# Unused pieces of 64 and 96 bytes between SBUF tiles in a decoder step: where matmul operands start modulo 128

## The chip, the cores and the metric

The kernel runs on one NeuronCore of one Trainium2 chip. The metric is the device time of one execution in microseconds (us). The engines are named as in the profile: PE is TensorE's matmul, PEld its weight load, DVE is VectorE, ACT is ScalarE, POOL is GpSimd, SP is the engine whose queue issues the DMAs. SBUF is the on-chip memory of 128 partitions; a tile has an address within the partition, the same in all 128, and that byte address is what this document is about.

## The reference

One inference step of a one-layer decoder, for 1024 prompt tokens and 64 sample tokens (8 sequences of 8), in float32:

```python
h = rmsnorm(x, norm_mix)
q, k, v, gu, gv, ga, gb = split_in(h @ w_in)          # 1024 -> 5120 columns
o  = sink_attention(q, k, v, ...)                     # window 128, 16 heads, 4 key heads
vn = layernorm(gelu(gv), ln_g, ln_b)
s  = spatial_gating(gelu(gu), vn, ws, bs)             # 6 groups of 128x128
x  = x + (sigmoid(ga) * (o @ w_pa) + sigmoid(gb) * (s @ w_pb)) @ w_out
z  = rmsnorm(x, norm_ffn) @ w_up                      # 1024 -> 5632 columns
c  = conv_b + sum(zp[:, j:j + T] * conv_w[j] for j in range(3))
a, b = split(c, 2)
y  = rmsnorm(x + (gelu(a) * b) @ w_down, norm_final)  # 2816 -> 1024
```

The outputs are y for both groups, the new key, value and convolution states, and vn of the samples.

## The kernel before

**Three products for one.** Every large operand is held as two float32r tiles, a high part and the remainder (th and tl, wh and wl, hh and hl). A float32 product is made of three matmuls, high by high, high by low and low by high, accumulated in PSUM. Each matmul loads its own 128x128 weights; the other operand, the moving one, has 256, 288, 320 or 512 columns of 4 bytes.

**Two token groups.** Group 0 holds the 64 samples and 512 prompt tokens (576), group 1 the other 512.

**The stages, in order of time**, each with its matmul line:

- Token-major projections (L511, in mm_tok): gv and v. Here the hidden state is the weights operand (pools hs0 for group 0, hs1 for group 1) and the projection's weights are the moving operand, 256 columns, in pool wide. Group 0 has 5 token blocks, group 1 has 4, each for 4 column blocks of 24 matmuls: 480 and 384 matmuls.
- The combined projection (L295, in Chain.product): q, k, gu and the gates, in 16 column pairs. A pair is a 2x2 block product in 7 products instead of 8, each of 12 matmuls for a group: group 0 with 288 columns from pool T0h, group 1 with 256 columns from pool T1h, 16 x 84 = 1344 matmuls each. Three pairs run for group 0 alone at the start of the stage and for group 1 alone at its end; between them the groups alternate, twelve matmuls of one and twelve of the other.
- Attention for group 0, then group 1 (scores L1155 with kst as moving operand and q as weights, both in pool kv; transposes L1182; values L1206), with pieces of the branch and merge products (L238, in mm3) put between the steps. L238 of group 0 runs 320 and 256 columns in turn (pools mlp0, act0, later hm0), of group 1 512 columns (mlp1, act1, later hm1).
- The merge of group 1 and the output projection (L238, hm0 from 726 to 776 us, hm1 from 784 us).
- The up-projection (L295 again, psu banks): 22 column pairs, group 0 with 288 columns from pool T0, group 1 with 256 columns from pool T1, 22 x 84 = 1848 matmuls each. DVE and ACT make the weight parts (L41, L177) and run the convolution (L1532 to L1534) beside it.
- The down-projection (L1651, in mm_dn): 7 passes over 11 column pairs, three matmuls of 288 columns and three of 256 in turn, both from pool tq; 924 of each.

The weights of L295, L238 and L1651 come from ring buffers in pool wp, made by ACT (high part) and DVE (low part) at L41.

**Where a tile lies.** A pool on the left side is put at the end of the left pools open at that moment; one on the right side is put below those open on the right. Inside a pool, a name's buffers are put one after another when the name is first used, in steps of 32 bytes. So what comes into a left pool moves all later names of that pool, and all pools opened on the left while it is open; the right pools (hs0, T0h, mlp0, act1, vv1, T0, tq) stay. An address is taken again by a later pool when a pool closes; the first access to the new tile then waits for the last accesses to the old tiles it overlaps.

Nearly all tile sizes are multiples of 128 bytes, so a pool's start decides the address modulo 128 of all its operands. wp starts at byte 2336, which is 32 modulo 128, and each of its matmul operands is at 32. The columns "before" are the addresses in the built program before; "after" adds the bytes of the diff by the rule above. Distance is moving operand less weights, modulo 128.

| matmuls | columns | weights | moving operand | distance before | after |
|---|---|---|---|---|---|
| L511, group 0 (480) | 256 | hs0, 96 | wide, byte 113024: 0 | 32 | 64 (wide at 32) |
| L511, group 1 (384) | 256 | hs1, byte 78208: 0 | wide: 0 | 0 | 64 (hs1 at 96, wide at 32) |
| L295, group 0 (1344) | 288 | wp, 32 | T0h, 96 | 64 | 64 |
| L295, group 1 (1344) | 256 | wp, 32 | T1h, byte 70016: 0 | 96 | 64 |
| L238, group 0, branch (288) | 320, 256 | wp, 32 | mlp0, 96 | 64 | 64 |
| L238, group 1, branch (144) | 512 | wp, 32 | mlp1, byte 145792: 0 | 96 | 64 |
| L238, group 0, merge (384) | 320, 256 | wp, 32 | act0, byte 70016: 0 | 96 | 64 |
| L238, group 1, merge (192) | 512 | wp, 32 | act1, 96 | 64 | 64 |
| L238, group 0, output (384) | 320, 256 | wp, 32 | hm0, byte 102784: 0 | 96 | 64 |
| L238, group 1, output (192) | 512 | wp, 32 | hm1, byte 70016: 0 | 96 | 64 |
| L1155 (224) | 256 | q in kv, 0 | kst in kv, byte 106880: 0 | 0 | 64 (kst at 96, q at 32) |
| L1206, group 0 (56) | 512 | vv0, 0 | at0, 32 | 32 | 96 |
| L1206, group 1 (64) | 512 | vv1, 96 | at1, 32 | 64 | 96 |
| L295, up, group 0 (1848) | 288 | wp, 32 | T0, 96 | 64 | 64 |
| L295, up, group 1 (1848) | 256 | wp, 32 | T1, byte 55584: 32 | 0 | 64 |
| L1651 (924 and 924) | 288, 256 | wp, 32 | tq, 96 | 64 | 64 |

**The lines the steps touch.** The matmul that most of the span consists of is in Chain.product:

```python
for kk in range(4):
    th, tl = (x[:, (0, 1, 2, 6, 3, 5, 4)[j]] for x in self.tx[kk])
    for i, (u, v) in enumerate(((wh, th), (wh, tl), (wl, th))):
        PE.matmul(ps, u[:, kk, :], v, start=first and kk + i == 0,
                  stop=kk == 3 and i == 2, skip_group_check=True)
```

Its moving tiles are made here for group 1, in the combined projection and in the up-projection:

```python
txa[1][kk] = tuple(t1h.tile([P, 7, 256], F32R, name=f"t{y}{kk}") for y in "hl")
tx[1][kk] = tuple(t1p.tile([P, 7, 256], F32R, name=f"t{y}1{kk}") for y in "hl")
```

The pools around the change are c1 (small constants and statistics, open during everything up to the up-projection), wide, kv, mlp1 and T1. All DMAs of these stages go through the queue of SP; the order on each engine is the order of the program text.

Of the kernel before, what the change touches and what calls it, by code (L numbers as in the profile page):

```python
# [6 lines left out]
F32 = mybir.dt.float32  # L7
# [8 lines left out]
P = 128  # L16
# [18 lines left out]
def layer(tc, a):  # L35
# [13 lines left out]
    with ExitStack() as top:  # L49
# [191 lines left out]
        W = Weights(top.enter_context(tc.tile_pool(name="wp", bufs=2)), 4, 4)  # L241
        W.sm = top.enter_context(tc.tile_pool(name="sm", bufs=2))

        tx = [{}, {}]
        tops = ExitStack()

# [2 lines left out]
        def right(stack, name, bufs=1):  # L249
            return stack.enter_context(tc.tile_pool(name=name, bufs=bufs, side="right", reuse_waits="tile"))  # L250
# [110 lines left out]
        with ExitStack() as ph1:  # L361
            c1 = ph1.enter_context(tc.tile_pool(name="c1", bufs=1))
# [31 lines left out]
            wide = {}  # L394
# [68 lines left out]

            rstg = [c1.tile([P, len(gr["toks"])], F32, name=f"rst{gr['g']}") for gr in groups]
            lnst = c1.tile([P, 9, 3, 6], F32, name="lnst")
            pso = ExitStack()
            psa = pso.enter_context(tc.tile_pool(name="psa", bufs=7, space=PSUM))

# [25 lines left out]
            gvp = pa0.enter_context(tc.tile_pool(name="gvp", bufs=4))  # L494
            hp1 = pa0.enter_context(tc.tile_pool(name="hs1", bufs=1))
            wide["pool"] = pa0.enter_context(tc.tile_pool(name="wide", bufs=2))
            hp0 = right(hs0o, "hs0")
            rsg = [pool.tile([P, gr["n"]], F32, name=f"rs{gr['g']}") for gr, pool in zip(groups, (c1, hp1))]
            hs = [[], []]
# [390 lines left out]
            kvo, kvp = ExitStack(), {}  # L890
# [3 lines left out]
            def operands(gr, kv):  # L894

                def go():
                    if kv == NKV:
                        if gr["g"] == 0:
                            operands(groups[1], 0)()
                        return  # L900
                    g, n = gr["g"], gr["n"]
                    at, nk = ((NS, 512), (448, 640))[g]
                    t = kvp["p"].tile([P, 2, 640], F32R, name="kst", bufs=2)[:, :, :nk]
                    gr["kst"][kv] = t
                    r = 64 * (kv % 2)
                    for o in (0, 64):
                        nc.sync.dma_start(t[o:o + 64].bitcast(F32), kd[kv // 2][r:r + 64, :, at:at + nk])
                    for c in (2 * kv, 2 * kv + 1):
                        q = gr["qt"][c] = kvp["p"].tile([P, 2, 512], F32R, name="q", bufs=4)
                        nc.sync.dma_start(q.bitcast(F32), qd[g][c][:, :, gr["soff"]:n])  # L910
                return go

            def prepare(gr):

                g = gr["g"]
                gr["kvo"] = ExitStack()
                vp = (gr["kvo"].enter_context(tc.tile_pool(name="vv0", bufs=1, reuse_waits="tile")) if g == 0
                      else right(gr["kvo"], "vv1"))
                gr["vst"], gr["dvst"] = {}, {}

                def value(name, src, i):
                    def go():
                        t = gr[name][i] = vp.tile([P, NKV, P], F32R, name=f"{name}{i}")
                        nc.sync.dma_start(t.bitcast(F32), src[i])
                    return go

                vs, ds = (((0, 1, 2), (1, 2, 3)), ((3, 4, 5, 6), (4, 5, 6, 7)))[g]
                return [operands(gr, 0)] * (1 - g) + [value("vst", vd, vs[0])] + [
                    x for i in range(len(ds)) for x in (
                        [value("vst", vd, vs[i])] * (i > 0) + [value("dvst", dvd, ds[i])])] + [operands(gr, 1)]  # L930
# [44 lines left out]
            kvp["p"] = kvo.enter_context(tc.tile_pool(name="kv", bufs=1, reuse_waits="tile"))  # L975
            prep = prepare(groups[0])
            m1 = mo[1].enter_context(tc.tile_pool(name="mlp1", bufs=1, reuse_waits="tile"))
            b_order = [(0, 0), (1, 0), (0, 1), (1, 1)] + [(c, g) for c in range(2, KD) for g in range(2)]
            sgs, bst = {}, {}

# [465 lines left out]
        def pool2(name, bufs, **kw):  # L1446
            return ph2.enter_context(tc.tile_pool(name=name, bufs=bufs, reuse_waits="tile", **kw))

        t1p = pool2("T1", 1)
        up = pool2("up", 2)  # L1450
        pse = ExitStack()
        psu = pse.enter_context(tc.tile_pool(name="psu", bufs=8, space=PSUM, reuse_waits="tile"))
# [437 lines left out]
```

## Time and profile before

| | |
|---|---|
| median of 3 runs | 1540.58 us (1537.99 to 1541.20) |
| the profiled execution | 1540.43 us, span 1538.7 us, granted clock 0.998 |
| PE busy, share of the span | 1524.6 us, 99%, 11528 matmuls |
| DVE busy | 1178.6 us, 77% |
| ACT busy | 851.4 us, 55% |
| DMA queue of SP, share of 16 engines | 55.3% |

A profile's matmul record runs from the start of a matmul to the modelled end of its results, and the next one starts long before. A group's "mean ns" is the length of that record. How fast matmuls follow one another is seen from a stretch of time and the number of matmuls in it, or from the starts in the timeline. A row of the view by stretches gives the stretch, its length, for each engine its busy time and number of instructions, then the granted clock, the share of the DMA engines and GB/s. A row of groups gives line, engine, operation, output and inputs, shape and count, then busy time and mean, then idle time before.

### The profile page before, as it was taken

The page shows a single profiled execution, that of the slowest core. Times are in us where ns is not written, and L with a number is a line of the kernel's source. Part 1 is how long each engine was busy: PE and PEld are TensorE (multiplying, and loading weights), DVE is VectorE, ACT ScalarE, POOL GpSimd, SP SyncE. Part 2 cuts the span into 40 slices and gives each one's busy share as a digit, 9 for nine tenths or more (in the row PEclk, how much of TensorE's full clock was granted, in tenths as well). Part 3 has the DMA queues.
Part 4 walks back from the last instruction along what each step waited for, and adds up shares of the span by engine and source line. Part 5 has one row for each costly group of instructions (what it writes and reads, how often), then busy time and mean ns, then how long its engine had stood idle before and what let it go on. Part 6 is the DMA issues. An engine that isn't in the chain of part 4 may idle for free.

```text
span 1538.7 us, 30106 instructions
## 1 busy us (share of the span) xinstructions
PE 1524.6 (99%) x11528; PEld 1483.3 (96%) x11528; DVE 1178.6 (77%) x1897; ACT 851.4 (55%) x1767; POOL 267.8 (17%) x382
## 2 busy tenths in 40 slices
PE   9999999999999999999999999999999999999997
PEld 8999999999998989988989999999999999999997
DVE  7798876755576877979568978898898878775686
ACT  7557666653455775764444554655555556453452
POOL 0001000110030222310234222332142222000002
PEclk9999999999999999999999999999999999999999
DMA  7687446764778757449977423332232216973363
GB/s 244 219 270 260 161 161 218 236 212 142 241 237 285 221 165 252 152 140 312 339 255 267 138 109 113 121 120 93 108 128 100 102 62 224 365 252 96 111 183 123
DMA packets 135231, 289.88 MB, mean 188 GB/s; under 512 B 15536, under 2 KB 36848, under 8 KB 135088
## 3 DMA queue, kind: packets, MB, share of 16 engines
q1 hardware_dynamic: 134944, 287.96, 55.3%
q8 instruction: 90, 1.47, 0.4%
q14 instruction: 53, 0.43, 0.1%
q10 hardware_dynamic: 144, 0.01, 0.0%
HBM read 198.97 MB, written 90.92 MB: 188 GB/s over the span
## 4 chain that ended last, share of the span: by engine, by line
PE 87%; DMA 4%; DVE 3%; issue 3%; ACT 2%; POOL 1%; SPq 0%; POOLq 0%; ACTq 0%; DVEq 0%
PE st L295 45%; PE mm L238 16%; PE dn L1651 13%; PE st L511 6%; PE po L1206 2%; PE sc L1155 2%; PE pt L1182 1%; DMA v<-gvd 1%; POOL x L1714 1%; PE mx L793 1%; DMA wl<-upd 1%; DVE wl L41 1%; DMA kd<-q 0%; DMA x<-xt 0%; ACT wh L41 0%
## 5 line engine op out<-in xcount | busy, mean ns | idle before, releaser
L295 PE MATMUL st<-th,wh 128*128 128x288 f32 (+1 forms) x2128 | 616.9, 290 | 1.6 <-ACT k L274 1.2
L295 PE MATMUL st<-tl,wh 128*128 128x288 f32 (+1 forms) x2128 | 615.3, 289 | 0.0
L295 PE MATMUL st<-th,wl 128*128 128x288 f32 (+1 forms) x2128 | 614.4, 289 | 0.0
L295 PEld LDWEIGHTS st<-th,wh 128*128 128x128 f32 x2128 | 402.8, 189 | 3.1 <-ACT k L274 2.2
L295 PEld LDWEIGHTS st<-th,wl 128*128 128x128 f32 x2128 | 402.8, 189 | 0.0
L295 PEld LDWEIGHTS st<-tl,wh 128*128 128x128 f32 x2128 | 402.7, 189 | 0.0
L41 ACT CAST wh<-wraw 128x512 fp32r<-128x512 f32 (+2 forms) x188 | 129.4, 700 | 92.8 <-PE mm L238 41.4
L1651 PE MATMUL dn<-th,wh 128*128 128x288 f32 (+1 forms) x616 | 177.5, 288 | 0.8 <-ACT zb L321 0.6
L1651 PE MATMUL dn<-th,wl 128*128 128x288 f32 (+1 forms) x616 | 177.3, 288 | 0.2 <-DVE wl L41 0.2
L1651 PE MATMUL dn<-tl,wh 128*128 128x288 f32 (+1 forms) x616 | 177.2, 288 | 0.0
L41 DVE TENSOR_TENSOR wl<-wraw,wh 128x512 fp32r<-128x512 f32 (+2 forms) x188 | 148.2, 802 | 24.8 <-ACT wh L41 22.3
L41 DVE TENSOR_TENSOR wl<-ws,wh 128x512 fp32r<-128x512 f32 x168 | 118.5, 716 | 54.2 <-ACT wh L41 53.4
L41 ACT CAST wh<-ws 128x512 fp32r<-128x512 f32 x168 | 102.5, 621 | 91.7 <-PE st L295 63.4
L1651 PEld LDWEIGHTS dn<-th,wh 128*128 128x128 f32 x616 | 115.8, 188 | 1.2 <-ACT zb L321 0.8
L1651 PEld LDWEIGHTS dn<-th,wl 128*128 128x128 f32 x616 | 115.9, 188 | 0.4 <-DVE wl L41 0.4
L1651 PEld LDWEIGHTS dn<-tl,wh 128*128 128x128 f32 x616 | 115.9, 188 | 0.0
L41 ACT CAST th<-traw 128x544 fp32r<-128x544 f32 (+1 forms) x85 | 54.5, 642 | 52.1 <-PE dn L1651 38.5
L511 PE MATMUL st<-w2h,hh 128*128 128x256 f32 x288 | 81.3, 284 | 1.5 <-ACT hh L46 0.7
L511 PE MATMUL st<-w2l,hh 128*128 128x256 f32 x288 | 81.0, 282 | 0.0
L511 PE MATMUL st<-w2h,hl 128*128 128x256 f32 x288 | 80.3, 282 | 0.2 <-DVE hl L47 0.2
L41 DVE TENSOR_TENSOR tl<-traw,th 128x544 fp32r<-128x544 f32 (+1 forms) x85 | 61.0, 721 | 23.1 <-ACT th L41 22.7
L281 POOL TENSOR_TENSOR z<-kn,k 128x288 f32<-128x288 f32 (+1 forms) x32 | 31.1, 975 | 244.0 <-ACT kn L276 236.6
(271 smaller groups left out, 2941.3 us busy)
## 6 DMA issues: line engine op xcount, KB each, us to landing
wraw<-wt SPq DMA_DIRECT2D x137, 512.0 KB
traw<-td SPq DMA_DIRECT2D x77, 272.0 KB
td<-za SPq DMA_DIRECT2D x22, 544.0 KB
q<-qd SPq DMA_DIRECT2D x16, 512.0 KB
upd<-hl SPq DMA_DIRECT2D x14, 512.0 KB
td<-t SPq DMA_DIRECT2D x11, 544.0 KB
wpart<-wt SPq DMA_DIRECT2D x22, 256.0 KB
qd<-q SPq DMA_DIRECT2D x8, 576.0 KB
```

The costliest lines, as they stand in the source:

```text
L41: for x in (S.copy(hi, src), V.tensor_sub(lo, src, hi.bitcast(F32))):
L238: PE.matmul(ps[:, lo:lo + c1 - c0], u[:, k, :], v[:, c0:c1], start=(k == 0 and i == 0), stop=(k == nk - 1 and i == 2))
L281: op(to, pick(x, to, lo, hi), pick(y, to, lo, hi))
L295: PE.matmul(ps, u[:, kk, :], v, start=first and kk + i == 0, stop=kk == 3 and i == 2, skip_group_check=True)
L511: PE.matmul(ps, u[:, lo:lo + P], v[:, k, :], start=k + i == 0, stop=k == KD - 1 and i == 2)
L793: PE.matmul(ps[:, P * i:P * i + P], vn[:, i], late["wst"][:, c, :], start=True, stop=True)
L1155: PE.matmul(ps[:, h, o0:256], q, kst[kv][:, e, k0:cur + P], start=e == 0, stop=e == 1)
L1182: PE.transpose(pt[:, h * P:h * P + P], s[:, h, 0:P], ident)
L1206: PE.matmul(po, v[:, kv, :], t, start=e == 0, stop=last)
L1651: PE.matmul(place(m, e), u[:, m, :], v[:, lo:hi], start=new and i + k == 0 and (e == 0 or m % 2 == 0), stop=i == NU - 1 and k == 2, skip_g ...
L1714: G.tensor_mul(xc, xc, rs)
```

## The change

Five unused tiles are allocated. Nothing reads or writes them, and no instruction is added. 96 bytes stand at the end of c1; 64 bytes stand first in wide, in mlp1 and in T1, and behind kst in kv. What is allocated after them lies that much further on.

```diff
+        gaps = iter(range(99))
+
+        def line(pool, n):
+
+            pool.tile([P, n // 4], F32, name=f"gap{next(gaps)}", bufs=1)
...
             lnst = c1.tile([P, 9, 3, 6], F32, name="lnst")
+            line(c1, 96)
...
             wide["pool"] = pa0.enter_context(tc.tile_pool(name="wide", bufs=2))
+            line(wide["pool"], 64)
...
                     gr["kst"][kv] = t
+                    if g == 0 and kv == 0:
+                        line(kvp["p"], 64)
...
             m1 = mo[1].enter_context(tc.tile_pool(name="mlp1", bufs=1, reuse_waits="tile"))
+            line(m1, 64)
...
         t1p = pool2("T1", 1)
+        line(t1p, 64)
```

## The prediction

> **What bounds the kernel now.** I read the page's shares first, then its chain, then TensorE's own waits, and last the pace of the matmuls stage by stage.
>
> ```profile
> span 1538.7 us, 30106 instructions
> ...
> PE 1524.6 (99%) x11528; PEld 1483.3 (96%) x11528; DVE 1178.6 (77%) x1897; ACT 851.4 (55%) x1767; POOL 267.8 (17%) x382
> ...
> PEclk9999999999999999999999999999999999999999
> ...
> PE 87%; DMA 4%; DVE 3%; issue 3%; ACT 2%; POOL 1%; SPq 0%; POOLq 0%; ACTq 0%; DVEq 0%
> ```
>
> TensorE has work in 99% of the span, at full granted clock, and is 87% of the chain that ends last. The longest entries among its waits are small:
>
> ```profile
> PE st L295 <- ACT k L274: 1.2, 2, 0.9
> PE st L566 <- DVE c_ones L69: 1.2, 1, 1.2
> PE st L511 <- ACT hh L46: 0.7, 1, 0.7
> ```
>
> So the time is the number of matmuls times the interval from one start to the next, and only a change of that interval can move the end by much. The groups of matmuls that the change touches, with one untouched group (L1651) for comparison; there are two further rows like each of L295's and L1651's, one per high/low product:
>
> ```profile
> L295 PE MATMUL st<-th,wh 128*128 128x288 f32 x1064 | 316.0, 297 | 1.6 <-ACT k L274 1.2 <-ACT kn L276 0.3
> ...
> L295 PE MATMUL st<-th,wh 128*128 128x256 f32 x1064 | 300.9, 283 | 0.0
> ...
> L1651 PE MATMUL dn<-th,wh 128*128 128x288 f32 x308 | 91.0, 295 | 0.2 <-ACT wh L41 0.2
> ...
> L1651 PE MATMUL dn<-th,wh 128*128 128x256 f32 x308 | 86.5, 281 | 0.6 <-ACT zb L321 0.6
> ...
> L511 PE MATMUL st<-w2h,hh 128*128 128x256 f32 x288 | 81.3, 284 | 1.5 <-ACT hh L46 0.7 <-ACT rst L478 0.4 <-ACT w2h L41 0.3
> ...
> L1155 PE MATMUL sc<-kst,q 128*128 128x256 f32 x224 | 31.5, 283 | 0.0
> ```
>
> The 280 to 297 ns are the length of one record, and records overlap, so this column is no pace. The pace is a stretch's length over its count. The next view cuts the span into stretches with one kind of work each. A window also counts the two matmuls begun before it, so I take two off each count.
>
> ```profile
> core 0: us, PE busy (x) PEld busy (x) DVE busy (x) ACT busy (x) POOL busy (x), PEclk, DMA share, GB/s
> 26.20:51.20 25.00, 25.00 (x215) 25.00 (x215) 19.00 (x33) 19.91 (x38) 0.00 (x0) 1.00 0.66 210
> 81.00:114.00 33.00, 33.00 (x277) 33.00 (x276) 31.33 (x55) 18.82 (x34) 0.00 (x0) 1.00 0.87 286
> 116.00:149.00 33.00, 33.00 (x251) 33.00 (x250) 26.82 (x43) 23.63 (x48) 6.30 (x6) 1.00 0.78 265
> 160.00:300.00 140.00, 140.00 (x1111) 140.00 (x1111) 99.78 (x165) 89.59 (x175) 13.96 (x14) 1.00 0.54 185
> 437.00:468.00 31.00, 31.00 (x261) 31.00 (x260) 23.76 (x38) 21.81 (x45) 13.44 (x25) 1.00 0.89 297
> 681.00:724.00 43.00, 43.00 (x186) 34.67 (x186) 37.77 (x54) 19.35 (x28) 0.00 (x0) 1.00 0.88 304
> 726.00:776.00 50.00, 50.00 (x377) 50.00 (x377) 27.75 (x32) 18.79 (x26) 10.37 (x8) 1.00 0.95 334
> 784.00:822.00 38.00, 38.00 (x164) 30.60 (x163) 33.78 (x41) 16.62 (x24) 16.67 (x13) 1.00 0.70 227
> ...
> 997.00:1120.00 123.00, 123.00 (x978) 123.00 (x977) 105.43 (x150) 65.01 (x130) 33.66 (x51) 1.00 0.29 110
> ...
> 1320.00:1470.00 150.00, 150.00 (x1205) 150.00 (x1204) 102.75 (x184) 69.06 (x122) 0.00 (x0) 1.00 0.60 195
> ```
>
> With the addresses of the section on the kernel before ("distance" is moving operand less weights, modulo 128), these stretches read:
>
> - 26 to 51, L511, group 0, 256 columns, distance 32: 25.00/213 = 117.4 ns.
> - 81 to 114, L511, group 1, the same line and shape, distance 0: 33.00/275 = 120.0 ns.
> - 116 to 149, L295, group 0 alone, 288 columns, distance 64: 33.00/249 = 132.5 ns.
> - 437 to 468, L295, group 1 alone, 256 columns, distance 96: 31.00/259 = 119.7 ns.
> - 160 to 300, L295, both groups half and half: 140.00/1109 = 126.2 ns, a pair 252.5.
> - 997 to 1120, L295 of the up-projection, both groups, the 256 columns at distance 0: 123.00/976 = 126.0 ns, a pair 252.0.
> - 1320 to 1470, L1651, 288 and 256 columns half and half, both at distance 64: 150.00/1203 = 124.7 ns, a pair 249.4.
>
> The last three are the argument. The shapes are the same, the 288-column half stands at distance 64 in all, and the pair is 2.6 to 3.1 ns shorter where the 256-column half does too. With 132.5 for the 288 columns, the 256-column interval is 249.4 - 132.5 = 116.9 ns at distance 64, against 119.5 and 119.7 elsewhere. The two L511 rows show a difference of the same size under one line and shape, between two weight addresses.
>
> **The change part by part.** It adds no instruction; it moves tiles by whole multiples of 32 bytes. Each term is matmuls times the fall of the interval.
>
> 1. *Up-projection, group 1* (gap ahead of T1, distance 0 to 64): 22 column pairs of 84 matmuls = 1848, pair 252.0 to 249.4, so 2.6 ns each: 4.8 us.
> 2. *Combined projection, group 1* (T1h, 96 to 64): 16 x 84 = 1344 at 119.7 to 116.9, so 2.8 ns (3.1 by the pair): 3.8 us.
> 3. *Token-major projections, group 1* (L511, hs1 and wide, 0 to 64): 384 at 120.0 to 116.9: 1.2 us. VectorE is busy 31.33 of 33.00 us there, so I keep 1.0. Group 0 (480, from 32 to 64) stands at 117.4 already: 0, bounds 0 and 480 x 0.5 = 0.2 us.
> 4. *L238, 320 and 256 columns* (act0 and hm0, 96 to 64, 384 matmuls each). The same line already runs at distance 64 with mlp0. The timeline of TensorE gives 18 matmuls, nine of each shape, from the first to the last of these starts, mlp0 first, then hm0:
>
> ```profile
> 516.44 0.69 PE L238 MATMUL mm<-s,wh 128*128 128x320 f32 x4
> ...
> 518.82 0.69 PE L238 MATMUL mm<-s,wh 128*128 128x320 f32 x4
> ...
> 739.82 0.43 PE L238 MATMUL mm<-ml,wh 128*128 128x320 f32 x2
> ...
> 742.22 0.43 PE L238 MATMUL mm<-ml,wh 128*128 128x320 f32 x2
> ```
>
>    2.38 against 2.40 us, 1.1 ns a matmul, times 768: 0.8 us (rows of 0.01 us leave 0.4 to 1.3).
> 5. *Scores* (L1155, kst 0 to 64): 224 matmuls with no stretch of their own; bounds 0 and the 3.1 ns of term 3, so 0 to 0.7; with half of that, 0.3 us.
> 6. *512 columns* (mlp1 and hm1, 96 to 64): 681 to 724 has distance 64 at 43.00/184 = 233.7 ns, 784 to 822 has distance 96 at 38.00/162 = 234.6. One count more or less is 1.4 ns, so the two are the same: 0, bounds 0 and 336 x 0.9 = 0.3 us. The 120 of L1206 (512 columns too) change distance both ways: 0.
> 7. *Other engines' operands.* ACT, VectorE and the queues find the same rows 64 to 224 bytes further on. VectorE's busiest stretch on the long path is 105.43 of 123.00 us (86%), so a slower move costs nothing until it is over 14% slower. Since the moved tiles keep almost all their former neighbours in time, waits for a reused address stay. I take 0.5 us off for gains that run into stalls of the stages with waits.
>
> Sum: 4.8 + 3.8 + 1.0 + 0.8 + 0.3 - 0.5 = 10.2 us. The profiled execution took 1540.43 us (span 1538.7), 0.15 under the median of 1540.58 of three, which spread from 1537.99 to 1541.2. So 1540.43 - 10.2 = **1530.2 us**.
>
> A rule speaks against all of it. The Trainium skill, "TensorE: Matmul & The Clock Gate", Part 2, step 1, says that weights and moving operand come in by two independent SBUF read ports, so that loading the next weights takes nothing from the running matmul; by it the sum would be 0 and the time 1540.4. The trace does not agree: the two L511 rows, 117.4 and 120.0 ns, differ in stage and address alone.
>
> **The rivals.**
>
> *A. No effect.* L1651 changes shape every three matmuls and its output tile with it, L295 every twelve; if that order and not the address makes 249.4 of 252.0, nothing happens: 1540.4 us. For it: no 256-column stretch at distance 64 stands alone. Against it: the L511 rows, whose order is the same, and L238's 2.38 and 2.40 us. The rule above ends here too.
>
> *B. The gaps do not land as reckoned.* If the 96 bytes at the end of c1 did not carry through to the pools above it (they count in steps of 32 bytes, so they should), terms 2 to 4 fall away. Terms 1 and 5 with their own gaps stay at most: 1540.4 - 5.1 = 1535.3 us.
>
> *C. Another engine takes the gain.* L511 group 1 has VectorE at 95% (31.33 of 33.00), and DMA stands at 0.87 to 0.95 in four rows (81, 437, 681, 726). If these places keep their pace, terms 2 to 4 lose what lies there: 1.0, then 264 of T1h's matmuls or 0.7, then 0.8: 1530.2 + 2.5 = 1532.7 us. In the up-projection nothing is so full.
>
> *D. Slower: transfers into the moved tiles.* The four rows last 33 + 31 + 43 + 50 = 157 us at a mean DMA share of 0.90. If transfers took 25% longer at the new addresses, the share would be 1.125 and the stretches 157 x 0.125 = 19.6 us longer: 1530.2 + 19.6 = 1549.8 us. It decides from about 1.19 on: 157 x (0.90 x 1.19 - 1) = 11 us eats the whole gain. Against it: GB/s over share is 329 and 334 at 81 and 437, where moved tiles are loaded, and 325 at 1320, where the tiles stand at 96 modulo 128 already.
>
> **How the numbers follow.** Forecast 0.78 (own range 1527 to 1533.5: the pair differences are good to 0.4 ns, which is 1.3 us on 3192 matmuls, terms 3 to 6 leave another 1.5, and the runs spread by 1.6 to either side); C 0.06, B 0.04, A 0.08, D 0.04. The range from 1526.8 to 1536.5 holds the first three, 0.88 less their tails; it leaves out A and D. A measurement here tells 0.2%, 3.1 us, from no change. Forecast, B and C lie beyond it: faster 0.88; A: same 0.08; D: slower 0.04.
>
> **What would show it.** In the changed kernel, both L295 stretches with two groups should fall to about 124.7 ns a matmul, L295's stretch with group 1 alone and L511 group 1 to about 117, while L1651, the 512 columns and group 0 alone (132.5) keep theirs. L295 at 126 still would mean A, T1 alone faster would mean B, and new idle time before TensorE with DMA near 1.0 would mean C or D. I am wrong if the pair stays at 252, or if 512-column stretches lengthen.

## The result, and the profile after

The changed kernel takes 1530.07 us (median of four runs, 1528.59 to 1532.04) against 1539.63 (four runs, 1537.99 to 1541.20): ratio 0.9939, 95% interval 0.9922 to 0.9956, so 9.4 us faster, 6.8 to 12.0. The forecast was 1530.2. The line numbers of the new program are higher by 6 to 12: L295 is now L301, L511 L519, L1155 L1166, L1651 L1663.

The page of the changed kernel, its first rows and its chain:

```profile
span 1526.9 us, 30105 instructions
...
PE 1513.9 (99%) x11528; PEld 1472.5 (96%) x11528; DVE 1177.8 (77%) x1897; ACT 851.1 (56%) x1767; POOL 266.8 (17%) x382
...
PE 88%; DVE 3%; issue 3%; ACT 2%; DMA 2%; POOL 1%; SPq 0%; POOLq 0%; ACTq 0%; DVEq 0%
```

Each of the five engines has the same number of instructions as before, TensorE is as full, and the span is 11.8 us shorter in this execution (it is the fastest of the four). VectorE and ACT are busy as long as before. The longest entries of TensorE's waits are as small as before:

```profile
PE st L574 <- DVE c_ones L69: 1.2, 1, 1.2
PE pt L1109 <- DVE s L1102: 0.7, 1, 0.7
PE pt L1193 <- DVE s L1186: 0.6, 2, 0.4
```

So the matmuls follow one another faster. The view by stretches of the changed kernel, columns as in the prediction, answers to the rows shown there; again two are taken off each count of PE:

```profile
26.20:51.20 25.00, 25.00 (x214) 24.90 (x212) 19.00 (x33) 19.65 (x38) 0.00 (x0) 1.00 0.65 207
81.00:113.00 32.00, 32.00 (x274) 32.00 (x273) 30.20 (x53) 18.45 (x34) 0.00 (x0) 1.00 0.85 282
116.00:148.00 32.00, 32.00 (x244) 32.00 (x243) 27.28 (x45) 23.35 (x47) 6.29 (x6) 1.00 0.81 280
160.00:300.00 140.00, 140.00 (x1129) 140.00 (x1128) 103.41 (x168) 94.69 (x185) 13.27 (x14) 1.00 0.57 192
431.00:460.00 29.00, 28.66 (x251) 28.46 (x250) 23.92 (x37) 20.68 (x43) 13.80 (x22) 1.00 0.88 301
673.00:717.00 44.00, 44.00 (x190) 35.29 (x189) 37.84 (x54) 19.20 (x27) 0.00 (x0) 1.00 0.86 299
718.00:767.00 49.00, 49.00 (x374) 49.00 (x373) 28.48 (x33) 19.43 (x26) 10.36 (x8) 1.00 0.92 330
775.00:813.00 38.00, 38.00 (x164) 30.64 (x163) 33.92 (x41) 17.25 (x24) 16.68 (x13) 1.00 0.70 227
987.00:1109.00 122.00, 122.00 (x977) 122.00 (x976) 106.30 (x151) 64.81 (x130) 34.44 (x51) 1.00 0.30 111
1300.00:1450.00 150.00, 150.00 (x1206) 150.00 (x1205) 99.91 (x177) 67.81 (x120) 0.00 (x0) 1.00 0.61 201
```

- L511, group 0: 25.00/212 = 117.9 ns (117.4 before).
- L511, group 1: 32.00/272 = 117.6 ns (120.0 before).
- Group 0 alone, 288 columns: 32.00/242 = 132.2 ns (132.5).
- Combined projection, both groups: 140.00/1127 = 124.2, a pair 248.4 ns (252.5).
- Combined projection, group 1 alone: 29.00/249 = 116.5 ns (119.7), with TensorE idle 0.34 us of the 29.00, where it was not idle before.
- L238 of 320 and 256 columns: 49.00/372 = 131.7 ns (133.3).
- L238 of 512 columns: 44.00/188 = 234.0 ns (233.7) and 38.00/162 = 234.6 ns (234.6).
- Up-projection: 122.00/975 = 125.1, a pair 250.3 ns (252.0).
- Down-projection, untouched: 150.00/1204 = 124.6, a pair 249.2 ns (249.4).

Where the 11.8 us of span lie, by the starts of each stage's first matmul in the two traces: up to the combined projection -1.0, combined projection -6.5 (353.5 to 347.1), attention with its products -0.2 (256.9 to 256.7), output projection -0.6, up-projection -4.4 (469.6 to 465.2), down-projection and end +0.8. These shares differ between executions: in a second trace of the changed kernel (below) the combined projection took 349.2 us, which is -4.3 against before.

### The profile page after: what moved, and what is told of

It is laid out like the page before. It is cut to its first block, busy times and chain, and to the rows that moved or that the text cites. A ratio compares the mean times of both kernels' runs of the same rounds, so it can differ in the third digit from the quotient of the medians.

```text
span 1526.9 us, 30105 instructions
## 1 busy us (share of the span) xinstructions
PE 1513.9 (99%) x11528; PEld 1472.5 (96%) x11528; DVE 1177.8 (77%) x1897; ACT 851.1 (56%) x1767; POOL 266.8 (17%) x382
## 4 chain that ended last, share of the span: by engine, by line
PE 88%; DVE 3%; issue 3%; ACT 2%; DMA 2%; POOL 1%; SPq 0%; POOLq 0%; ACTq 0%; DVEq 0%
PE st L301 48%; PE mm L238 15%; PE dn L1663 13%; PE st L519 6%; PE po L1217 2%; PE sc L1166 1%; PE pt L1193 1%; DVE wl L41 1%; PE mx L801 1%; ACT s L1183 1%; POOL x L1726 1%; DMA x<-xt 0%; DMA vnd<-v 0%; DMA stg<-sd 0%; ACT wh L41 0%
## 5 line engine op out<-in xcount | busy, mean ns | idle before, releaser
L301 PE MATMUL st<-th,wh 128*128 128x288 f32 (+1 forms) x2128 | 612.7, 288 | 0.7 <-ACT k L280 0.6
L301 PE MATMUL st<-tl,wh 128*128 128x288 f32 (+1 forms) x2128 | 611.1, 287 | 0.0
L301 PE MATMUL st<-th,wl 128*128 128x288 f32 (+1 forms) x2128 | 609.5, 287 | 0.0
L301 PEld LDWEIGHTS st<-th,wh 128*128 128x128 f32 x2128 | 400.0, 188 | 1.7 <-ACT k L280 1.3
L301 PEld LDWEIGHTS st<-th,wl 128*128 128x128 f32 x2128 | 400.8, 188 | 0.0
L301 PEld LDWEIGHTS st<-tl,wh 128*128 128x128 f32 x2128 | 399.3, 188 | 0.0
L1663 PE MATMUL dn<-th,wh 128*128 128x288 f32 (+1 forms) x616 | 177.3, 288 | 0.8 <-ACT zb L327 0.6
L1663 PE MATMUL dn<-th,wl 128*128 128x288 f32 (+1 forms) x616 | 177.0, 287 | 0.2 <-DVE wl L41 0.2
L1663 PE MATMUL dn<-tl,wh 128*128 128x288 f32 (+1 forms) x616 | 176.9, 287 | 0.0
L1663 PEld LDWEIGHTS dn<-th,wh 128*128 128x128 f32 x616 | 115.7, 188 | 1.2 <-ACT zb L327 0.8
L1663 PEld LDWEIGHTS dn<-th,wl 128*128 128x128 f32 x616 | 115.8, 188 | 0.4 <-DVE wl L41 0.4
L1663 PEld LDWEIGHTS dn<-tl,wh 128*128 128x128 f32 x616 | 115.7, 188 | 0.0
L519 PE MATMUL st<-w2h,hh 128*128 128x256 f32 x288 | 80.9, 283 | 0.7 <-ACT rst L485 0.4
L519 PE MATMUL st<-w2l,hh 128*128 128x256 f32 x288 | 80.5, 280 | 0.0
L519 PE MATMUL st<-w2h,hl 128*128 128x256 f32 x288 | 79.7, 280 | 0.2 <-DVE hl L47 0.2
```

The lines of the kernel that those rows point to most:

```text
L301: PE.matmul(ps, u[:, kk, :], v, start=first and kk + i == 0, stop=kk == 3 and i == 2, skip_group_check=True)
L519: PE.matmul(ps, u[:, lo:lo + P], v[:, k, :], start=k + i == 0, stop=k == KD - 1 and i == 2)
L1663: PE.matmul(place(m, e), u[:, m, :], v[:, lo:hi], start=new and i + k == 0 and (e == 0 or m % 2 == 0), stop=i == NU - 1 and k == 2, skip_g ...
```

## The experiments

"Interval" below is the mean from one matmul's start to the next one's in the trace, in one stage, without those over 1.25 times the median (the stalls); a stage's stretch is given beside it where it carries the verdict. Distances are moving operand less weights, modulo 256 unless said otherwise.

### One gap alone

```diff
-            line(c1, 96)
...
-            line(wide["pool"], 64)
...
-                    if g == 0 and kv == 0:
-                        line(kvp["p"], 64)
...
-            line(m1, 64)
...
         line(t1p, 64)
```

> Only the 64 bytes ahead of T1; everything else as in the kernel before. Distance theory (what counts is moving operand less weights, modulo 128): the up-projection's 256-column interval falls from 119.9 to 117 or 118 ns on 1848 matmuls, 3.5 to 4.8 us, so a time of about 1535.5 us, and the combined projection keeps 252.5 ns a pair. No-effect theory (order of the matmuls, not addresses): 1539.6 us and 252.0 ns a pair in the up-projection.

1536.84 us against 1540.8, ratio 0.9978 (0.9969 to 0.9988): 3.4 us. A stretch of the up-projection in the kernel before, and then the same stretch with T1's gap alone:

```profile
1000.00:1105.00 105.00, 105.00 (x835) 105.00 (x834) 89.66 (x126) 56.98 (x114) 27.96 (x40) 1.00 0.28 104
```

```profile
1000.00:1105.00 105.00, 105.00 (x840) 105.00 (x840) 91.34 (x127) 57.76 (x116) 28.22 (x40) 1.00 0.29 104
```

105.00/833 = 126.05 ns becomes 105.00/838 = 125.30, so a pair falls by 1.5 ns in this stretch; by starts, over the whole stage, T1's interval falls from 119.7 to 117.5 ns, and T1h's stays (119.8). The no-effect theory is out: 64 unused bytes, no other edit, and the pace of one stage changes.

The counterpart keeps c1's 96 bytes and drops the other four:

> Only the 96 bytes at the end of c1; the other four gaps undone. Distance theory, modulo 256: T1h at 192 falls from 119.8 to 115.7 ns (1344 matmuls, 5.5 us), act0 and hm0 at 192 fall by 1 ns at 256 and 2 ns at 320 columns (768 matmuls, 1.2 us), the token-major stage comes to distance 0 for both groups (group 0 up from 117.7 to 119.9, 480 matmuls, 1.1 us worse), T1 stays at 119.7: 5.6 us in all, ratio 0.9964. With the 3.4 us of T1 alone that leaves 0.5 us of the whole change's 9.5 for wide, kv and mlp1. Modulo 128 alone: T1h falls to T1's 117.5 ns only (3.1 us), ratio 0.998.

1536.37 us against 1539.51, ratio 0.9980 (0.9971 to 0.9990). The paces came as expected modulo 256 (T1h 115.9, the token-major stage 120.0 in both groups, T1 119.7), but the time gained only 3.1 us of the 5.6. By the time alone the reading modulo 128, which expected 0.998, would have been right; T1h's pace, 115.9 where it expected 117.5, rules it out. In this trace, 4.3 us shorter than the one of before, only the combined projection falls short: it is 4.0 us shorter, where T1h's pace is worth 5.5 (token-major stage +1.1, attention -0.4, output projection -0.6). T1h's interval with the stalls left in is 118.0 ns, 2.1 over its stall-free pace, against 1.1 in the kernel before, which is 1344 x 1.0 = 1.3 us more of stalls. That these come from the change is not shown: the two traces of the changed kernel give 0.8 and 2.0 ns in the same place. In the stretch with group 1 alone TensorE is idle 0.11 us of 30.00, where it was not idle before, and the DMA engines stand at 0.91:

```profile
435.00:465.00 30.00, 29.89 (x258) 29.57 (x258) 24.16 (x38) 21.53 (x44) 14.06 (x24) 1.00 0.91 303
```

The rest of the shortfall is inside the interval of the ratio.

### The weights moved instead

```diff
         W = Weights(top.enter_context(tc.tile_pool(name="wp", bufs=2)), 4, 4)
+        line(W.pool, 64)
         W.sm = top.enter_context(tc.tile_pool(name="sm", bufs=2))
+        line(W.sm, 64)
```

(on the kernel before, without the five gaps)

> 64 bytes ahead of the weight rings and 64 behind them, so that the weights move to 96 modulo 128 and every moving operand stays where it was before. Distance theory: T1 comes to distance 64 and T1h to 160 (about 117.5 ns, down 2.4 on 3192 matmuls, 7.6 us less), while the 288 columns of T0h, T0 and tq go to 0 and 128 and their 132.5 ns rise to about 135 (4116 matmuls, 11 us more) and tq's 256 columns from 117 to 119.9 (2.7 us more): slower, about 1546 us. Position theory (what counts is where the moving operand alone stands, 96 good, 0 and 32 bad): no stage changes its pace, 1539.6 us.

1536.12 us against 1540.8, ratio 0.9966 (0.9955 to 0.9976): faster, where the distance theory as I had it said slower. The same stretch of the up-projection and a stretch of the down-projection in this kernel:

```profile
1000.00:1105.00 105.00, 105.00 (x839) 105.00 (x839) 91.07 (x127) 58.28 (x117) 27.54 (x40) 1.00 0.29 104
```

```profile
1298.00:1468.00 170.00, 170.00 (x1366) 170.00 (x1365) 118.50 (x206) 76.51 (x135) 0.00 (x0) 1.00 0.64 206
```

The position theory is out too: modulo 128, T1 lies where it lay in the kernel before, and its interval is 117.6 ns, the number it has when T1 is moved and the weights are not. Modulo 256 T1 did move, from 32 to 160, because the two gaps together shift the pools above them by 128 bytes. The kernel u1 below settles that: it has T1 at 160 too, with the weights at 32 instead of 96, and its interval there is 119.4 ns. The same place of the moving operand gives two paces, so the weights' place counts. T1h, at 160, runs at 118.3. What failed is the extension to 288 columns. T0's stand at 0 or 128 now and take 131.7 and 134.1 ns, where 64 and 192 gave 132.5 and 132.7; on the mean nothing like 135. The down-projection's 170.00/1364 = 124.6 ns is what it was: its 256 columns take 116.4 ns at 0 and 119.1 at 128, instead of 118.3 at 64 and 116.2 at 192.

### All eight distances

The first sweep gave the eight tiles of T1, and those of T1h, eight distances within one stream:

```diff
+                    if kk or y == "l":
+                        line(t1p, 32)
+                    pair_.append(t1p.tile([P, 7, 256], F32R, name=f"t{y}1{kk}"))
```

(T1h the same, after 192 bytes)

> Every tile of T1 and T1h starts 32 bytes further than the one before it, so that the eight tiles of each stage stand at the eight distances 0 to 224 from the weights modulo 256; nothing else is changed. Distance theory: intervals of matmuls by distance of about 119.9 at 0, 117.5 at 64, 120.0 at 96, 117.6 at 160, 115.8 at 192, and the same list from both stages although the tiles of a distance differ; 32, 128 and 224 are new. No-effect theory: 119.9 for all eight. Time between 1535 and 1540 us by either.

1535.55 us in one run. The list did not come: distance 0 gave 117.8 and 117.5 ns instead of 119.9, 192 gave 116.6 and 117.7 instead of 115.8, and T1h's and T1's numbers at one distance lie up to 2 ns apart (128: 116.6 and 118.6). In a stream whose distance changes from matmul to matmul, the interval is not that of the matmul's own distance. So the next three kernels gave each stage one distance for all its matmuls, by one gap at the start of its pool:

```diff
+            line(wide["pool"], 128)
...
+            line(t1h, 32)
...
+        line(t1p, 128)
```

(u1; u2 and u3 the same with other lengths. In u1 and u2 also 128 bytes behind each tile of T0, and in u2 64 more behind the last.)

> The kernel before with T1 at distance 128 (modulo 256), T1h at 128, hs1/wide at 128 and hs0/wide at 32, each the same for all matmuls of its stage; and 128 unused bytes behind each tile of T0, so that the up-projection's 288 columns keep one distance (192 or 64) within each product of 12 matmuls instead of changing it from tile to tile. If the interval goes by the distance modulo 128, 128 gives the 119.7 to 120.0 ns of distance 0 in T1, T1h and hs1 alike; if modulo 256 it can be another number, but the same one within 0.5 ns in the three stages. T0: if mixed distances blur an effect that 288 columns have as well, the even products (192) fall by 1.5 ns or more below 132.5 and the odd ones (64) do not; if 288 columns are insensitive to distance, all stay at 132.5.

> The kernel before with T1 at distance 32, T1h and hs1/wide at 224, hs0/wide at 128, and T0 as in the kernel u1 but 64 bytes lower, so that its 288 columns stand at 128 or 0, one distance within each product. Distance theory: T1h and hs1 agree within 0.5 ns; hs0 at 128 agrees with the other stages at 128. By the token-major stage's 116.8 ns at 32 in the kernel with the moved weights, T1 comes to about 117. T0: if 288 columns have the effect, 135 ns at distance 0; if they are insensitive, 132.5.

> The kernel before with T1 at distance 160, T1h at 32, hs1/wide at 96 and hs0/wide at 0. Distance theory: T1 118 (T1h's 118.3 at 160 in the kernel with the moved weights), T1h the number of T1 at 32 in the kernel u2, hs1 120 as T1h at 96 before, hs0 120 as hs1 at 0 before. Theory that stage and stream matter more than the distance: the pairs of stages differ by more than 1 ns at one distance.

One run each: 1538.56, 1535.62 and 1540.63 us, beside 1539.93 for the kernel before. The intervals of 256 columns in streams of one distance, in ns, from all kernels of this document:

| distance | T1 | T1h | L511, hs1 | L511, hs0 |
|---|---|---|---|---|
| 0 | 119.7 | | 120.0 | 120.0 (u3) |
| 32 | 117.0 (u2) | 117.1 (u3) | | 117.6 (u1), 116.8 (moved weights) |
| 64 | 117.5 | | 117.8 | 117.9 |
| 96 | | 119.8 | 120.0 (u3) | |
| 128 | 119.4 (u1) | 118.8 (u1) | 118.7 (u1) | 119.6 (u2) |
| 160 | 118.5 (u3) | 118.3 (moved weights) | | 117.7 |
| 192 | 115.9 (192 throughout) | 115.7 | 114.2 (192 throughout) | 116.4 (192 throughout) |
| 224 | | 118.2 (u2) | 118.3 (u2) | |

Stages agree within about 1 ns at each distance but 192; the 0.5 ns that u1 and u2 asked for at 128 was missed (118.7 to 119.6). Between traces with one distance T1's number varies by 0.2 ns, that of hs0 by 0.7 (117.7 to 118.3 at 160). By the means of the rows, 64 and 192 differ by 2.2 ns, 96 and 224 by 1.7, 32 and 160 by 1.0 and 0 and 128 by 0.8. The two larger differences are beyond the scatter: it goes by 256, not by 128. A period of 512 does not show: group 0 of L511 has weights at two places 256 bytes apart modulo 512, and they take 119.98 and 119.95 ns at distance 0 (u3), 116.5 and 116.3 at 192. u2's stretch shows the best of the new ones, T1 at 32, 105.00/842 = 124.7 ns:

```profile
1000.00:1105.00 105.00, 105.00 (x844) 105.00 (x843) 91.26 (x129) 57.24 (x114) 28.02 (x40) 1.00 0.29 104
```

T0 with one distance in each product: 133.0 ns at 192, 132.0 at 64 (u1), 133.2 at 128 and 131.5 at 0 (u2): neither of the outcomes that u1 and u2 named. So 288 columns are not quite insensitive, but their spread is 1.7 ns where that of 256 columns is about 4, and 192, the best there, is not the best here.

### 192 throughout

```diff
-            line(wide["pool"], 64)
+            line(wide["pool"], 192)
...
-        line(t1p, 64)
+        line(t1p, 192)
```

> The change with 192 instead of 64 bytes in wide and T1, so that every 256-column operand stands 192 instead of partly 64 bytes off the weights modulo 256. If only the distance modulo 128 counts: as the change, 1530.1 us. If it counts modulo 256, as the combined projection's 115.8 ns at 192 against the up-projection's 117.5 ns at 64 in the changed kernel suggest: T1 falls by another 1.7 ns on 1848 matmuls (3.1 us) and the token-major projections by up to 1.7 on 864 (1.5 us), so about 1526 us.

1525.36 us against 1540.8, ratio 0.9904 (0.9890 to 0.9919). T1 fell to 115.9, the token-major stage to 114.2 (group 1) and 116.4 (group 0). Group 1 of the token-major stage and the up-projection in this kernel:

```profile
79.00:111.00 32.00, 32.00 (x285) 32.00 (x284) 30.58 (x54) 19.07 (x34) 0.00 (x0) 1.00 0.85 281
```

```profile
1000.00:1105.00 105.00, 105.00 (x847) 105.00 (x846) 89.88 (x128) 56.66 (x114) 25.32 (x41) 1.00 0.29 106
```

32.00/283 = 113.1 ns, where the change has 117.6; 105.00/845 = 124.3 ns, where it has 105.00/838 = 125.3. Group 1's 114.2 is a mean of two paces: by blocks of 24 matmuls, all run at 113.3 to 113.5 ns but the second to fifth, which take 117.5 to 121.2. The last kernel does the same for the down-projection, and ran beside the changed kernel on one chip:

```diff
-                raw = dnp["t"].tile([P, HT], F32, name="traw", bufs=4)
+                raw = dnp["t"].tile([P, 576], F32, name="traw", bufs=4)[:, :HT]
...
-                th, tl = (dnp["t"].tile([P, HT], F32R, name=x, bufs=5) for x in ("th", "tl"))
+                th, tl = (dnp["t"].tile([P, 576], F32R, name=x, bufs=5)[:, :HT] for x in ("th", "tl"))
...
             t_upto(4, 2)
+            line(dnp["t"], 128)
```

> The changed kernel itself, for comparison on one chip with the next: ratio 0.994 to the kernel before. T1 at 117.5 ns, T1h at 115.8.

> The kernel far192, and in the down-projection each tile of tq widened from 544 to 576 columns and 128 bytes more behind them, so that its 256 columns always stand at 192 and its 288 columns at 64 (before, each at 64 or 192 in turn). Distance theory: the 256 columns of the down-projection go from 117.2 to 116.2 ns on the mean (924 matmuls, 0.9 us), the 288 columns stay at 132.2; far192's ratio 0.9904 becomes 0.990, against 0.994 of the change. If the two kinds of distance in turn were as good, 0.9904.

The change again: 1531.54 us against 1539.51, ratio 0.9947 (0.9935 to 0.9960), T1 at 117.8 and T1h at 116.0 ns. With 192 throughout and the down-projection: 1522.62 us, ratio 0.9887 (0.9872 to 0.9902), the fastest of all, and clear of the change. From 192 throughout without the down-projection (0.9890 to 0.9919) it is not clear by the time, so that step is read from its stage. The down-projection's 256 columns went to 114.4 ns, not 116.2: the stretch gives 167.00/1355 = 123.2 ns against 124.6.

```profile
1287.00:1454.00 167.00, 167.00 (x1357) 167.00 (x1356) 116.99 (x204) 75.50 (x134) 0.00 (x0) 1.00 0.64 208
```

Before, each of its tiles stood at 64 or 192 in turn, and those at 192 took 116.2 ns; with all of them at 192 they take 114.4. Here a steady distance is worth more than its own number in a mixed stream; at 0 it was the other way round (119.7 steady, 117.5 and 117.8 mixed).

## Why the prediction was right, and where it was not

The time and its sign were right, and so was the ground: TensorE's pace is the time, the pace of 256-column matmuls goes by the distance of their two operands, and little else in the kernel took the gain. That was read from a pair of stages and a pair of groups in the kernel before; the experiments with one gap and with the moved weights show it. That 1530.2 came within 0.2 us of the measured median is luck: the gain is known to 2.6 us either way, and measured again it was 8.2 us. The table below sets the terms beside what the two profiled executions gave (interval by interval, times the same counts). These two differ by 11.8 us, more than the 9.4 of the ratio, and part of that is fewer stalls among 288-column matmuls, which the change does not touch: T0's interval with the stalls left in fell from 133.3 to 132.9 ns, 0.7 us on 1848.

| term | predicted, us | measured, us |
|---|---|---|
| 1, up-projection | 4.8 | 1848 x (119.95 - 117.97, stalls left in) = 3.7; T1 alone, by the clock, 3.4 |
| 2, combined projection, group 1 | 3.8 | 1344 x (119.8 - 115.7) = 5.5; with the stalls left in 6.0, and 4.0 in the second trace of the changed kernel |
| 3, L511, group 1 | 1.0 | 384 x (120.0 - 117.8) = 0.8 |
| 4, L238, 320 and 256 | 0.8 | 1.1 |
| 5, scores | 0.3 | 224 x (118.7 - 115.6) = 0.7 |
| 6, 512 columns | 0 | 0.4 or less (mlp1 234.8 to 232.3 ns, 144; hm1 233.4 to 233.3) |
| stalls taken off | -0.5 | about -1.4 in attention: it gained 0.2 of some 1.6 that terms 4 to 6 have there; the scores kept their 0.7, act0 lost its 0.5 to longer stalls |

**Terms 1 and 2 were mis-sized, one up and one down, and their errors largely cancel.** I took one price for distance 64 modulo 128, 116.9 ns, from the down-projection. That stage runs half at 64 and half at 192 modulo 256, and 116.9 was a mean of two numbers, 118.3 and 116.2. T1 came to 64 (117.5 by starts), T1h to 192 (115.7), and so did act0, hm0 and the scores. The kernel with 192 throughout shows that the split was there to be taken: 1525.36 us.

**Group 0 of L511** was put at no gain, and had none: 117.7 to 117.9 ns; 160, where it stood, is as good as 64.

**Term 7** gives VectorE a margin of 14% in the up-projection; 123.00/105.43 makes it 17%. The margin was not needed: VectorE was busy 1177.8 us instead of 1178.6.

**Term 4's price** (1.1 ns from two rows of 2.38 and 2.40 us) measured 1.0 and 0.9 ns at 256 columns and 1.6 and 2.4 ns at 320, for act0 and hm0.

**The rule of two independent read ports** (the Trainium skill, "TensorE: Matmul & The Clock Gate", Part 2, step 1) would have given 1540.4 us. The runs do not agree with it as a rule of time: T1's gap alone, one edit of 64 bytes, is 3.4 us. Whether the two reads disturb each other, or something else makes the difference, no run here shows.

**The rivals.** A (order, not address) fell with the single gap and the moved weights. B did not occur: the bytes of c1 carried through to T1h, whose pace changed in its run alone. C is seen in small: in the changed kernel's stretch with group 1 alone TensorE stands idle 0.34 us, 0.3 of it in one wait for ACT's copy of k, and in attention act0's faster matmuls were followed by as much waiting. D did not occur: its four stretches moved 282, 301, 299 and 330 GB/s at DMA shares of 0.85, 0.88, 0.86 and 0.92 in the change, against 286, 297, 304 and 334 at 0.87, 0.89, 0.88 and 0.95 before. The distance theory itself had a wrong step behind the prediction, that 288 columns suffer at 0 as 256 do; that cost the expectation of the moved weights its sign.

## What to carry to other kernels

Where TensorE is busy all the time, read its pace (stretch over count) by stage and by shape: two stages of one shape whose paces differ by 2% are a lead, and the operands' byte addresses belong in the comparison. Here 256-column float32r matmuls ran at 114 to 120 ns depending on moving operand less weights modulo 256, best in the projections with a steady 192; a few unused bytes ahead of a pool set it, and cost no time that shows here. Measure a sweep with one distance per stream, since tiles at mixed distances hide the effect.

## What the runs showed of the hardware that was not expected

- The distance counts modulo 256 (0, 32, 64, 96, 128, 160, 192, 224: about 119.9, 117.1, 117.7, 119.9, 119.1, 118.2, 115.5, 118.2 ns for 256 columns, means of the table's rows).
- It is a property of the stream, not of a matmul: a matmul at 0 among others at 32 to 224 takes 117.8 ns, among its like 119.7. With T1 at 192, the twelve matmuls of a product, which follow twelve of 288 columns, start at 118 to 120 ns and go on, from the sixth, at 114 to 115 (means over the stage's products). The timeline of TensorE in the kernel with 192 throughout, the first, the fifth and the last of one product:

```profile
1012.60 0.28 PE L301 MATMUL st<-th,wh 128*128 128x256 f32 x1
...
1013.08 0.28 PE L301 MATMUL st<-tl,wh 128*128 128x256 f32 x1
...
1013.87 0.28 PE L301 MATMUL st<-th,wl 128*128 128x256 f32 x1
```

  Four intervals in 0.48 us, then seven in 0.79 us. At distance 0 most stay at 119 to 121 ns, and T1h at 96 goes back and forth between some 117 and 124.
- Neighbouring columns differ: 320 profits (hm0 147.8 ns at 96 and 145.5 at 192; with the moved weights 147.2 at 160, and mlp0 144.1 at 128), 288 less (131.4 to 134.1 over all distances and streams), 512 hardly (act1 and hm1 233.3 or 233.4 at 96, 128 and 192, 234.3 at 160; mlp1's shorter runs 232.3 at 64, 234.8 at 96). In L238, where 320 and 256 columns take turns, 192 is not the best for 256: hm0 took 117.9 ns there and 116.1 at 160, in the kernel with the moved weights.
- What mechanism sets the pace, and whether a matmul's own weights or those loaded for the next one count, stays open: within each stage all weights had one address modulo 256, so no run here tells them apart.
